# Written order for z and for attention's output product, the last head's outputs split from PSUM, and one conv step per product

## The chip, the cores and the metric

The kernel runs on one core of one Trainium2 chip. The metric is device time in microseconds, the median of three runs. Five engines work side by side and meet through semaphores: PE (TensorE, the matmuls), DVE (VectorE), ACT (ScalarE), POOL (GpSimd) and SP (SyncE, which here only issues transfers). PEld in the profile is PE's loading of stationary operands.

## The reference, cut to what matters

The kernel computes one layer of a decoder block on a sequence of 1024 tokens of width 1024, all in float32: a Mamba-2 branch and a differential-attention branch side by side, merged by gates, and then a gated feed-forward with a causal convolution of width 3.

```python
proj = h @ w_in[layer]
z, xbc, dt_raw, q, k, v, gates = jnp.split(proj, IN_SPLITS, axis=-1)
y_ssd = ssd_branch(z, xbc, dt_raw, ...)      # uses silu(z), dt = softplus(dt_raw + dt_bias), decays exp(cumsum(dt * a))
y_att = diff_attention_branch(q, k, v, ...)  # 8 heads: softmax 1 - lam * softmax 2, times v, then an RMS norm
gate_ssd, gate_att = jnp.split(jax.nn.sigmoid(gates), N_BRANCH, axis=-1)
merged = gate_ssd * (y_ssd @ w_ssd_o[layer]) + gate_att * (y_att @ w_attn_o[layer])
mix = merged @ w_out[layer]
...
u = causal_dwconv(h2 @ w_up[layer], conv_ffn_w[layer], conv_ffn_b[layer])
u_gate, u_val = jnp.split(u, 2, axis=-1)
f = (jax.nn.gelu(u_gate, approximate=True) * u_val) @ w_down[layer]
```

## The kernel before, in words

**Products in three parts.** Every large product keeps float32 accuracy by splitting each operand into a high part (rounded, type `fp32r`) and a low part (what is left), and adding three matmuls: high x high, high x low, low x high. `split(hi, lo, raw)` does this with one ACT instruction (line 93) and one DVE instruction (line 94). `mm3` (lines 112 to 117) issues the three matmuls for each of a list of operand pairs. Raw weights land in three rotating buffers (`wraw`), their high and low parts in four each (`whi`, `wlo`); a buffer is free again when all that reads it is done. PSUM has two double banks for products (`ps_mm`), two single banks `wa` and one each of `wb` and `wc`.

**Who sets the order.** Outside of `tc.manual_schedule(engines=...)` a scheduler orders each engine's instructions by a cost model; within it, the named engines run them in the order in which the program writes them.

**z (lines 522 to 543).** The product for z and dt is cut into three thirds of some 346 columns. A third loads four weight slices (`wz`, two blocks of 128 rows each) and runs eight products of 24 matmuls, one for each 128 tokens. Each product's sixth and last group of matmuls by slice reads slice 3. A product is evacuated by a tanh on ACT (539), a multiply-add on DVE (540) and a store to `zd` (541). POOL works meanwhile on sums of down-projection weights (`down_sums`, lines 411 to 420): two 512 KB loads, four sums, two 512 KB stores, once for every four products. After the first third, `decays` (line 482 on) computes softplus and the decays from the 16 dt columns: a chain of some twenty small DVE steps, then two matmuls (`acum_ps`), exponentials, and eight transposes. All of this is ordered by the scheduler.

**Attention (lines 1126 to 1166).** 64 items (8 heads x 8 query blocks) run in written order on PE, DVE, ACT and POOL; SP is left to the scheduler. For an item, `scores` makes the two score products, `probs` the softmax pair `p` (1069), `transposes` turns `p` (1077) and copies it to `aT` (1078), and `values` multiplies by v (1090). Between these, `fill` emits one piece at a time of other products (here the gate product `gap`), and `run_bg` emits small steps that wait in a list. After every fourth item `norm_o` queues the RMS norm of the outputs (its steps on `sqt` are lines 1099 to 1108) and `out_o` transposes them, scales them to `osb` and stores them to DRAM (`atd`, lines 1117 to 1119).

**Attention's output product.** After the last item come 36 turns with a call of `fill` each (the last 20 pieces; then it has nothing left), the last `out_o` among them. Beside them the 16 parts of the attention output (8 blocks x 2 halves of the tokens) are loaded back from `atd` into `stg` (1178) and split into `oT`, one every second call, the last part only at the end. Then eight output blocks `ao` of 48 matmuls each follow, in scheduler's order: load and split the block's weight (`wao`), in blocks 1, 2 and 6 `early_sums` (load two feed-forward weights, make four sums on DVE, lines 1228 to 1231, and store them from POOL, 1233 and 1234), in blocks 3 to 6 the splits of a quarter of `w_out`, the loads of the gate and the Mamba state, two halves of matmuls, and the merge (`mt`, 1256 and 1257, and the split into `mT`).

**Feed-forward up.** The up product goes by pairs of blocks m, each with seven products p of 12 matmuls (`up_mms`, lines 1356 to 1358) on PSUM banks X, Y and Z, by a scheme with seven products where eight would be usual. Behind each product stand, in written order, sums of banks (`cg`, `cv`, on DVE at 1780, 1789 and 1793; `evs` copies on ACT), sums and splits of coming weights, and steps of the convolution of the block before: `up_conv(m, 0..3)` is a multiply-add over 1022 or 1023 columns on DVE (1374, with an ACT step ahead of every second), `up_conv(m, 4)` the product of gate and value (1378), and `up_gsum(m, 0..3)` four sums of 512 columns (1392). The table `convs` says behind which product (m, p) each stands.

**From up to down.** The down product needs left factors (`left_part`: load and split the stored activations, `g_hi` and `g_lo`) and right factors (`right_part`: load and split weights, `wdb`). The first ones are prepared behind the last up block's products 3 to 6, the later ones in the quarters q of the down product's steps kp.

Of the kernel before, what the change touches and what calls it, by code (L numbers as in the profile page):

```python
# [61 lines left out]
def kernel(ctx: ExitStack, tc: tile.TileContext, a: dict, out: bass.AP, dbg=None):  # L62
# [20 lines left out]
    def ps_wa(name):  # L83
        return pp.tile([P, HALF], F32, tag="wa", name=name, bufs=2)
# [37 lines left out]
    def new_hl(name):  # L122
        return SL.get(name, F32R, (P, 2, HALF))
# [358 lines left out]
    def decays():  # L482
        CH = 8 * NH
        f = lambda t: t.rearrange("p c h -> p (c h)")
# [17 lines left out]
        V.scalar_tensor_tensor(la, dt, -1.0, aexp[:, None, :].broadcast_to([P, 8, NH]), op0=ALU.mult, op1=ALU.mult)  # L502
        pa = ps_wa("acum_ps")
# [10 lines left out]
        V.tensor_tensor(acx[:, :, NH:], acum, hi_r.bitcast(F32), op=ALU.subtract)  # L514
        V.memset(acT.bitcast(F32), 0.0)
# [6 lines left out]
    for c0, wdt in ((0, 346), (346, 346), (692, 348)):  # L522
        wz = [load_moving(a["w_zdt"], 2 * kp, 2, c0, wdt, f"wz{c0}_{kp}") for kp in range(4)]
        for i in range(8):
            ps = ps_mm(f"z{c0}_{i}")[:, 0, :wdt]
            half, q = divmod(i, 4)
            if q == 0:
                down_sums(n_dn)
                n_dn += 1
            tsl = slice(q * P, (q + 1) * P)  # L530
            mm3(ps, [((hT[k][half][:, 0, tsl], hT[k][half][:, 1, tsl]), (wz[k // 2][0][:, k % 2, :], wz[k // 2][1][:, k % 2, :])) for k in range(KD)])
            lo = 0
            if c0 == 0:
                lo = NH
                V.tensor_tensor(dtr[:, i, :], ps[:, :NH], rows[:, R_DTB : R_DTB + NH], op=ALU.add)
            e = ev[n_ev % 2]
            n_ev += 1
            n = wdt - lo
            A.activation(e[:, 0, :n], ps[:, lo:], AF.Tanh, scale=0.5)
            V.scalar_tensor_tensor(e[:, 1, :n], e[:, 0, :n], 1.0, ps[:, lo:], op0=ALU.add, op1=ALU.mult)  # L540
            SP.dma_start(zd[i][:, c0 + lo - NH : c0 + lo - NH + n], e[:, 1, :n])
        if c0 == 0:
            decays()
# [569 lines left out]
    def out_o(j, grp):  # L1113
        need(("norm", j, grp))
        ptr = ps_wb(f"ot{j}_{grp}")
        for qi in range(4):
            T.transpose(ptr[:, qi * P : (qi + 1) * P], ob[:, qi, :], ident)
        A.activation(oe, ptr, AF.Copy, scale=subw)
        SP.dma_start(atd[j][:, grp * HALF : (grp + 1) * HALF], oe)

# [5 lines left out]
    with tc.manual_schedule(engines={EN.PE, EN.DVE, EN.Activation, EN.Pool}):  # L1126
# [6 lines left out]
        for t, (j, i) in enumerate(items):  # L1133
# [28 lines left out]
            emitted["values"] += 1  # L1162
            if j < 7 and i == (4 if j == 0 else 3):
                load_heads(j + 1)
# [5 lines left out]
        SL.put(*thl[0], *thl[1], *qst[0], *kst[0], *klo[0], vt[0], *pt_[0], *qst[1], *kst[1], *klo[1], *pt_[1], vt[1], *aTs)  # L1170

        oT = [[None] * 2 for _ in range(KD)]
        stg = [SL.get(f"stg{i}", F32, (P, 2, HALF)) for i in range(2)]
        parts = [(k, half) for half in range(2) for k in range(KD)]

        def att_in(n):
            k, half = parts[n]
            SP.dma_start(stg[n // 2 % 2][:, n % 2, :], atd[k][:, half * HALF : (half + 1) * HALF])

        def att_split(n):  # L1180
            k, half = parts[n]
            st = stg[n // 2 % 2][:, n % 2, :]
            oT[k][half] = new_hl(f"oT{k}_{half}")
            split(oT[k][half][:, 0, :], oT[k][half][:, 1, :], st)
            if n + 4 < len(parts) - 1:
                att_in(n + 4)

        for n in range(4):
            att_in(n)
        n_att = 0  # L1190
# [9 lines left out]
        while n_att < len(parts) - 1:  # L1200
            att_split(n_att)
            n_att += 1
        att_in(len(parts) - 1)
        att_split(len(parts) - 1)
    SL.put(osb, gev, *stg)
    for k in range(KD):
        SL.put(*hT[k])
    if dbg is not None and "att" in dbg:
        for j in range(8):
            SP.dma_start(dbg["att"][j], atd[j])  # L1210
    if dbg is not None and "ms" in dbg:
        for j in range(8):
            SP.dma_start(dbg["ms"][j], msd[j])


    mT = [[new_hl(f"mT{k}_{h}") for h in range(2)] for k in range(KD)]
    wo = [[None] * 4 for _ in range(2)]
    KH = KD // 2
    fbs = [h * KF + k for k in range(KF) for h in range(2)]

    wsd = [[dp.tile([P, 2, HALF], F32, tag=f"wsd{m}_{i}", name=f"wsd{m}_{i}") for i in range(2)] for m in range(3)]

    def early_sums(m):
        ra, rb = [wp.tile([P, 2, HALF], F32, tag="wraw", name=f"ws{m}_{i}", bufs=3) for i in range(2)]
        for r_, b in ((ra, fbs[m]), (rb, NFF + fbs[m])):
            SP.dma_start(r_.rearrange("p h c -> p (h c)"), a["w_up"][b])
        a11, a12, a21, a22 = ra[:, 0], ra[:, 1], rb[:, 0], rb[:, 1]
        V.tensor_tensor(a22, a21, a22, op=ALU.add)
        V.tensor_tensor(a21, a11, a21, op=ALU.subtract)
        V.tensor_tensor(a11, a22, a11, op=ALU.subtract)  # L1230
        V.tensor_tensor(a12, a12, a11, op=ALU.subtract)
        for i, (x_, y_) in enumerate(((a11, a22), (a21, a12))):
            G.dma_start(wsd[m][i][:, 0], x_)
            G.dma_start(wsd[m][i][:, 1], y_)

    gth = SL.get("gth2")
    mst = SL.get("mst")
    mt = SL.get("mt")
    for j in range(8):
# [3 lines left out]
        if 3 <= j < 7:  # L1243
            kp = j - 3
            raw = wp.tile([P, 2, HALF], F32, tag="wraw", name=f"wo1_{kp}_raw", bufs=3)
            SP.dma_start(raw, a["w_out"][2 * kp * P : (2 * kp + 2) * P, HALF:].rearrange("(k p) c -> p k c", p=P))
            wo[1][kp] = (new_hl(f"wo1_{kp}_hi"), new_hl(f"wo1_{kp}_lo"))
            split(*wo[1][kp], raw)
        ps = ps_mm(f"ao{j}")
        SP.dma_start(gth, gad[j])  # L1250
        SP.dma_start(mst, msd[j])
        for half in range(2):
            block_half(ps[:, half, :], w, oT, half)
        for half in range(2):
            hsl = slice(half * HALF, (half + 1) * HALF)
            V.scalar_tensor_tensor(mt[:, hsl], gth[:, hsl], 1.0, ps[:, half, :], op0=ALU.add, op1=ALU.mult)
            V.tensor_tensor(mt[:, hsl], mt[:, hsl], mst[:, hsl], op=ALU.add)
            split(mT[j][half][:, 0, :], mT[j][half][:, 1, :], mt[:, hsl])
# [231 lines left out]
    with tc.manual_schedule(engines={EN.PE, EN.DVE, EN.Activation, EN.Pool}):  # L1490
# [249 lines left out]
        for (m, p), c in {  # L1740
            (2, 2): (),
            (2, 3): ((0, 2), (0, 3)),
            (2, 4): ((0, 4),),
            (2, 5): ((1, 0),),
            (2, 6): ((1, 1), (1, 2)),
            (3, 0): ((1, 3), (1, 4)),
            (3, 1): (),
            (3, 2): (),
            (3, 3): ((2, 0),),
            (3, 4): ((2, 1), (2, 2)),  # L1750
            (3, 5): ((2, 3),),
            (3, 6): ((2, 4),),
        }.items():
            convs[m, p] = [(up_conv, *x_) for x_ in c]
        convs[3, 1] = [(up_gsum, 1, i) for i in range(2)]
        convs[3, 2] = [(up_gsum, 1, i) for i in range(2, 4)]
        for m in range(2, NPAIR):
# [4 lines left out]
            for p in range(2 if m == 2 else 0, 7):  # L1762
# [183 lines left out]
```

## Time and profile before

| | |
|---|---|
| median of 3 runs | 1925.46 us (1922.19 to 1927.95) |
| profiled execution | 1931.72 us, span 1929.6 us, mean granted TensorE clock 0.994 |
| PE busy | 1868.5 us, 97% of the span, 9128 matmuls |
| DVE, ACT, POOL busy | 1203.8, 852.9 and 214.0 us |
| bytes moved | 310.53 MB, 161 GB/s over the span |
| where the stages lie (us of the span) | z 215 to 325; last scores and probabilities up to 1074; output product 1093 to 1190; early up blocks 1320 to 1380; up to down 1680 to 1720 |

A line of the profile names the source line, the engine, the operation, the output and input by the program's names, and the shapes. In a timeline the first number is the start and the second the time that the instruction, or a group of like ones, took; the bracket tells how long the engine had been idle before, and what it waited for. A row of waits has the total, the number of times and the longest. Rows of instruction groups have busy time and mean duration in ns, and then the idle time before them. Rows of issues have the size and the median time from issue to landing.

### The profile page before, as it was taken

To read this page: it belongs to the slowest core of one execution; us is meant where nothing else is said; L and a number is where in the kernel's file an instruction comes from. 1 tells how busy PE (TensorE), PEld (TensorE's weight loads), DVE (VectorE), ACT (ScalarE), POOL (GpSimd) and SP (SyncE) were. 2 spreads that over 40 slices of the span, in tenths; PEclk is the share of its full clock that TensorE was granted. 3 is DMA by queue.
4 is the path that set the end of the run, shared out by engine and by line. 5 is a ranking of instruction groups with operands and counts; after the bars stand their busy time and mean duration, and the time that the engine had idled before them with its cause. 6 is when DMAs were issued, how large, how long until landed. Compare 5 with 4: busy or idle time off the path is not lost.

```text
span 1929.6 us, 24511 instructions
## 1 busy us (share of the span) xinstructions
PE 1868.5 (97%) x9128; PEld 1556.7 (81%) x9128; DVE 1203.8 (62%) x1815; ACT 852.9 (44%) x1630; POOL 214.0 (11%) x225
## 2 busy tenths in 40 slices
PE   6999989999999999999999899999999999999998
PEld 4787988888888888888888688887788888878886
DVE  6957343575226227767666553468988888886545
ACT  6522123555223115556556432365545455465532
POOL 0000252454451000000000100100000000000001
PEclk9999999999999999999999999999999999999999
DMA  9834364132766846665651776122322232278754
GB/s 303 276 113 148 117 229 164 66 115 88 264 217 142 262 152 178 162 176 160 167 162 58 234 246 207 55 77 77 129 96 104 106 119 93 104 231 282 245 158 158
DMA packets 136151, 310.53 MB, mean 161 GB/s; under 512 B 17120, under 2 KB 48480, under 8 KB 136032
## 3 DMA queue, kind: packets, MB, share of 16 engines
q1 hardware_dynamic: 128384, 282.70, 46.1%
q0 software_dynamic: 7648, 26.26, 4.0%
q8 instruction: 72, 1.18, 0.2%
q14 instruction: 47, 0.39, 0.1%
HBM read 219.49 MB, written 89.41 MB: 160 GB/s over the span
## 4 chain that ended last, share of the span: by engine, by line
PE 82%; DVE 6%; DMA 5%; ACT 4%; issue 2%; SPq 1%; POOL 0%; POOLq 0%; ACTq 0%; DVEq 0%
PE upx L1357 4%; PE upx L1358 4%; PE upx L1356 4%; PE o L1090 3%; PE dx L1720 2%; PE dx L1721 2%; PE dx L1719 2%; PE xbc L117 2%; PE xbc L116 2%; PE xbc L115 2%; PE upy L1357 2%; PE upy L1356 2%; PE upy L1358 2%; PE dy L1721 2%; PE dy L1720 2%; PE dy L1719 2%
## 5 line engine op out<-in xcount | busy, mean ns | idle before, releaser
L1356 PE MATMUL upx<-t,wu_t 128*128 128x512 f32 x264 | 103.4, 392 | 3.4 <-DVE cv L1789 3.0
L1357 PE MATMUL upx<-t,wu_t 128*128 128x512 f32 x264 | 102.9, 390 | 0.2 <-DVE t L1474 0.2
L1358 PE MATMUL upx<-t,wu_t 128*128 128x512 f32 x264 | 102.8, 389 | 0.0
L1078 ACT COPY aT<-at 128x512 f32<-128x512 f32 (+2 forms) x96 | 46.2, 481 | 110.5 <-PE at L1077 110.5
L1330 ACT ACTIVATE wu_t<-sab 128x512 fp32r<-128x512 f32 x57 | 34.0, 627 | 125.7 <-DVE sab L1347 125.7
L1090 PEld LDWEIGHTS o<-vt,aT 128*128 128x128 f32 x576 | 74.8, 191 | 9.5 <-ACT aT L1078 5.3
L1090 PE MATMUL o<-vt,aT 128*128 128x128 f32 x576 | 80.8, 276 | 0.3
L94 DVE TENSOR_TENSOR g_lo<-gst,g_hi 128x1024 fp32r<-128x1024 f32 (+1 forms) x42 | 47.6, 1134 | 49.2 <-ACT g_hi L93 49.2
L142 POOL TENSOR_TENSOR rsf<-rsf,nhalf 128x1 f32<-128x1 f32 x8 | 5.6, 704 | 631.1 <-DVE rsf L141 628.3
L115 PE MATMUL z<-wz_hi,hT 128*128 128x346 f32 (+1 forms) x192 | 63.7, 334 | 9.9 <-ACT wz_hi L93 9.5
L93 ACT ACTIVATE g_hi<-gst 128x1024 fp32r<-128x1024 f32 (+1 forms) x42 | 41.6, 990 | 70.5 <-DMA gst<-gld_s 33.0
L1051 DVE TENSOR_REDUCE nmx<-sc 128x1 f32<-128x640 f32 (+3 forms) x64 | 65.6, 1025 | 2.1
L142 POOL TENSOR_TENSOR sqt<-sqt,nhalf 128x4 f32<-128x4 f32 x16 | 16.5, 1033 | 441.3 <-DVE sqt L141 441.2
L1031 PE MATMUL sc<-kst,qst 128*128 128x512 f32 (+2 forms) x192 | 63.8, 340 | 0.0
L115 PE MATMUL xbc<-hT,wx_hi 128*128 128x512 f32 x160 | 63.5, 397 | 0.0
L116 PE MATMUL z<-wz_lo,hT 128*128 128x346 f32 (+1 forms) x192 | 63.2, 329 | 0.0
L1032 PE MATMUL sc<-klo,qst 128*128 128x512 f32 (+2 forms) x192 | 63.2, 346 | 0.0
L117 PE MATMUL z<-wz_hi,hT 128*128 128x346 f32 (+1 forms) x192 | 62.8, 327 | 0.0
L117 PE MATMUL xbc<-hT,wx_lo 128*128 128x512 f32 x160 | 62.3, 389 | 0.0
L116 PE MATMUL xbc<-hT,wx_hi 128*128 128x512 f32 x160 | 62.2, 389 | 0.0
L1356 PEld LDWEIGHTS upx<-t,wu_t 128*128 128x128 f32 x264 | 49.6, 188 | 15.4 <-DVE cv L1789 4.3
L1374 DVE SCALAR_TENSOR_TENSOR ug<-cg,vec,ug 128x1023 f32<-128x1023 f32 (+1 forms) x44 | 56.3, 1280 | 6.3 <-ACT ug L1373 5.1
(447 smaller groups left out, 5850.5 us busy)
## 6 DMA issues: line engine op xcount, KB each, us to landing
adas<-in_w_ada SPq DMA_DIRECT2D x32, 512.0 KB, 5.1
wdr<-in_w_down POOLq DMA_DIRECT2D x22, 512.0 KB, 6.9
wtd<-wds POOLq DMA_DIRECT2D x22, 512.0 KB, 4.4
wuf<-in_w_up SPq DMA_DIRECT2D x22, 512.0 KB, 3.5
gld_s<-gsum SPq DMA_DIRECT2D x22, 512.0 KB, 2.8
gst<-gld_s SPq DMA_DIRECT2D x20, 512.0 KB, 4.7
wdt_raw<-wtd SPq DMA_DIRECT2D x20, 512.0 KB, 4.5
wuv<-in_w_up SPq DMA_DIRECT2D x19, 512.0 KB, 3.6
```

The costliest lines, as they stand in the source:

```text
L115: T.matmul(ps, lh, rh, start=(i == 0), stop=False)
L116: T.matmul(ps, lh, rl, start=False, stop=False)
L117: T.matmul(ps, ll, rh, start=False, stop=(i == n - 1))
L1031: T.matmul(sc[:, n0:n1], qs_[s][:, tsl], ks_[s][:, n0:n1], start=True, stop=False)
L1051: V.reduce_max(nmx[:, bq, s : s + 1], sc[:, :L], axis=AX.X, negate=True)
L1090: T.matmul(po_of[j, grp][:, qi, :], at[:, k, :], vt[j % 2][:, kt, :], start=(kt == 0), stop=(kt == i))
L1356: T.matmul(out_, wh, xh_, start=(k == 0 and first), stop=False, skip_group_check=not first)
L1357: T.matmul(out_, wh, xl_, start=False, stop=False, skip_group_check=not first)
L1358: T.matmul(out_, wl, xh_, start=False, stop=(k == end), skip_group_check=not first)
L1719: T.matmul(o, gh[:, kk, tsl], wh, start=(k == 0 and not more), stop=False, skip_group_check=more)
L1720: T.matmul(o, gh[:, kk, tsl], wl, start=False, stop=False, skip_group_check=more)
L1721: T.matmul(o, gl[:, kk, tsl], wh, start=False, stop=(k == KF - 1), skip_group_check=more)
```

## The change

- **z.** The z loop is put under written order for PE, DVE, ACT and SP. A third's first three weight slices are fetched behind product 1 of the third before; all four are split behind its product 7, ahead of that product's evacuation, and the fourth is fetched once the first is split. `decays` is cut in three, placed behind products 1, 3 and 5 of the second third.
- **Last head.** At item 55 slots are freed and the loads of stored parts start; from item 57 on, one or two parts are split after each item, ten in all. Head 7 is no longer stored: `out_o` splits its two halves from PSUM. 20 turns are left, four splits stand beside them, and the first output weight is fetched and split there.
- **Output product.** It moves into the written order of PE, DVE, ACT and POOL. Each block's weight is split half a block ahead and fetched one and a half blocks ahead. `early_sums` stands in blocks 0, 1 and 2.
- **Up.** The steps of the convolution for blocks 0 to 4 go one by one behind the 25 products from (2, 3) to (5, 6), with four sums joined to others.
- **Down.** Behind the last up block's products 4, 5 and 6 stand left 0, right 0 and left 1; in the down product, a right part stands in quarter 0 and a left part in quarter 1.

```diff
-    for c0, wdt in ((0, 346), (346, 346), (692, 348)):
-        wz = [load_moving(a["w_zdt"], 2 * kp, 2, c0, wdt, f"wz{c0}_{kp}") for kp in range(4)]
...
+    z_raw = [fetch_z(*thirds[0], kp) for kp in range(3)]
+    with tc.manual_schedule(engines={EN.PE, EN.DVE, EN.Activation, EN.SP}):
+        for t_, (c0, wdt) in enumerate(thirds):
...
+                if t_ < 2 and i == 1:
+                    z_raw = [fetch_z(*thirds[t_ + 1], kp) for kp in range(3)]
+                if t_ < 2 and i == 7:
+                    wz_next = []
+                    for kp in range(4):
+                        wz_next.append(split_z(*thirds[t_ + 1], kp, z_raw.pop(0)))
+                        if kp == 0:
+                            z_raw.append(fetch_z(*thirds[t_ + 1], 3))
...
+                if t_ == 1 and i in (1, 3, 5):
+                    (decays_a, decays_b, decays_c)[i // 2]()
...
+        if j == KD - 1:
+            o = oT[j][grp] = new_hl(f"oT{j}_{grp}")
+            A.activation(o[:, 0, :], ptr, AF.Copy, scale=subw)
+            V.scalar_tensor_tensor(o[:, 1, :], ptr, subw, o[:, 0, :].bitcast(F32), op0=ALU.mult, op1=ALU.subtract)
+            return
...
+            if t == 55:
+                SL.put(*thl[0], *thl[1], *qst[0], *kst[0], *klo[0], vt[0])
+                stg = [SL.get(f"stg{i}", F32, (P, 2, HALF)) for i in range(2)]
+                for _ in range(4):
+                    att_in()
+            elif t > 56:
+                for _ in range(2 if i % 2 else 1):
+                    if n_att < 10:
+                        att_split()
...
-        for n in range(16 + NLAST):
-            if n == 12:
+        for n in range(NLAST):
+            if n == 11:
                 out_o(*pend)
+            if n == 1:
+                fetch_ao(0)
             fill(1)
             run_bg(1)
-            if n % 2 == 1 and n >= 5 and n_att < len(parts) - 1:
-                att_split(n_att)
-                n_att += 1
+            if n % 2 == 1 and n < 9:
+                att_split()
+            if n == 13:
+                split_ao(0)
...
-        w = load_block(a["w_attn_o"][j], f"wao{j}")
-        if j in (1, 2, 6):
-            early_sums(min(j - 1, 2))
...
+        fetch_ao(1)
+        for j in range(KD):
+            w = w_ao.pop(j)
+            ps = ps_mm(f"ao{j}")
+            SP.dma_start(gth, gad[j])
+            SP.dma_start(mst, msd[j])
+            block_half(ps[:, 0, :], w, oT, 0)
+            split_ao(j + 1)
+            fetch_ao(j + 2)
+            if j < 3:
+                early_sums(j, *early_load(j))
...
+            block_half(ps[:, 1, :], w, oT, 1)
...
-        convs = {(m, p): [(up_conv, m - 1, p)] for m in range(3, NPAIR) for p in range(5)}
-        for m in range(4, NPAIR, 2):
+        convs = {(m, p): [(up_conv, m - 1, p)] for m in range(6, NPAIR) for p in range(5)}
+        for m in range(6, NPAIR, 2):
...
-            (2, 3): ((0, 2), (0, 3)),
-            (2, 4): ((0, 4),),
-            (2, 5): ((1, 0),),
-            (2, 6): ((1, 1), (1, 2)),
-            (3, 0): ((1, 3), (1, 4)),
-            (3, 1): (),
-            (3, 2): (),
-            (3, 3): ((2, 0),),
-            (3, 4): ((2, 1), (2, 2)),
...
+        early = [(up_conv, 0, i) for i in range(2, 5)] + [(up_conv, 1, i) for i in range(4)]
+        early = [[x_] for x_ in early] + [[(up_conv, 1, 4), (up_gsum, 1, 0)], [(up_gsum, 1, i) for i in range(1, 4)]]
+        early += [[(up_conv, 2, i)] for i in range(5)] + [[(up_conv, 3, i)] for i in range(4)]
+        early += [[(up_conv, 3, 4), (up_gsum, 3, 0)], [(up_gsum, 3, 1), (up_gsum, 3, 2)], [(up_conv, 4, 0), (up_gsum, 3, 3)]]
+        early += [[(up_conv, 4, i)] for i in range(1, 5)]
+        for n, x_ in enumerate(early):
+            convs[2 + (n + 3) // 7, (n + 3) % 7] = x_
...
-                    if p >= 3:
-                        left_part(0, p - 3)
-                    if p >= 5:
-                        wd[p - 5] = right_part(0, p - 5)
+                    if p in (4, 6):
+                        left_part(0, p // 2 - 2)
+                    elif p == 5:
+                        wd[0] = right_part(0, 0)
...
-                if q == 0 and kp + 4 < KP:
-                    left_part(0, kp + 4)
+                if q == 0 and kp + 1 < KP:
+                    wd[kp + 1] = right_part(0, kp + 1)
                 elif q == 1 and kp + 2 < KP:
-                    wd[kp + 2] = right_part(0, kp + 2)
+                    left_part(0, kp + 2)
```

More of the change, by code (lines that the diff above doesn't have):

```diff
@@ L480, with decays_a @@
     aexp = const("aexp", [P, NH])
[L482 to L484 removed]
+    CH = 8 * NH
+    f = lambda t: t.rearrange("p c h -> p (c h)")
+    def decays_a():
         t0 = f(sp0_)
@@ L520, in decays @@
             V.tensor_copy(acT[:32, half * HALF : (half + 1) * HALF], pt[:32, :])
-    for c0, wdt in ((0, 346), (346, 346), (692, 348)):
-        wz = [load_moving(a["w_zdt"], 2 * kp, 2, c0, wdt, f"wz{c0}_{kp}") for kp in range(4)]
[L524 to L543, printed above, removed]
+    thirds = ((0, 346), (346, 346), (692, 348))
@@ new lines, in fetch_z, with split_z @@
+    def fetch_z(c0, wdt, kp):
+        raw = wp.tile([P, 2, wdt], F32, tag="wraw", name=f"wz{c0}_{kp}_raw", bufs=3)
+        SP.dma_start(raw, a["w_zdt"][2 * kp * P : (2 * kp + 2) * P, c0 : c0 + wdt].rearrange("(k p) c -> p k c", p=P))
+        return raw
+    def split_z(c0, wdt, kp, raw):
+        hi = wp.tile([P, 2, wdt], F32R, tag="whi", name=f"wz{c0}_{kp}_hi", bufs=4)
+        lo = wp.tile([P, 2, wdt], F32R, tag="wlo", name=f"wz{c0}_{kp}_lo", bufs=4)
+        split(hi, lo, raw)
+        return hi, lo
@@ L1169 @@
                 pend = None
[L1170 to L1186, printed above, removed]
@@ L1199 @@
         run_bg(len(bg))
[L1200 to L1239, printed above, removed]
-        w = load_block(a["w_attn_o"][j], f"wao{j}")
-        if j in (1, 2, 6):
-            early_sums(min(j - 1, 2))
[L1243 to L1258, printed above, removed]
+        assert n_att == len(parts)
@@ new lines, with early_load @@
+        SL.put(osb, gev, *stg)
+        for k in range(KD):
+            SL.put(*hT[k])
+        mT = [[new_hl(f"mT{k}_{h}") for h in range(2)] for k in range(KD)]
+        wo = [[None] * 4 for _ in range(2)]
+        KH = KD // 2
+        fbs = [h * KF + k for k in range(KF) for h in range(2)]
+        wsd = [[dp.tile([P, 2, HALF], F32, tag=f"wsd{m}_{i}", name=f"wsd{m}_{i}") for i in range(2)] for m in range(3)]
+        def early_load(m):
+            ra, rb = [wp.tile([P, 2, HALF], F32, tag="wraw", name=f"ws{m}_{i}", bufs=3) for i in range(2)]
+            for r_, b in ((ra, fbs[m]), (rb, NFF + fbs[m])):
+                SP.dma_start(r_.rearrange("p h c -> p (h c)"), a["w_up"][b])
+            return ra, rb
@@ new lines, in early_sums @@
+        def early_sums(m, ra, rb):
+            a11, a12, a21, a22 = ra[:, 0], ra[:, 1], rb[:, 0], rb[:, 1]
+            V.tensor_tensor(a22, a21, a22, op=ALU.add)
+            V.tensor_tensor(a21, a11, a21, op=ALU.subtract)
+            V.tensor_tensor(a11, a22, a11, op=ALU.subtract)
+            V.tensor_tensor(a12, a12, a11, op=ALU.subtract)
+            for i, (x_, y_) in enumerate(((a11, a22), (a21, a12))):
+                G.dma_start(wsd[m][i][:, 0], x_)
+                G.dma_start(wsd[m][i][:, 1], y_)
@@ new lines @@
+        gth = SL.get("gth2")
+        mst = SL.get("mst")
+        mt = SL.get("mt")
+        fetch_ao(1)
[9 more added lines that the diff above has]
+                early_sums(j, *early_load(j))
+            elif j < 7:
+                kp = j - 3
+                raw = wp.tile([P, 2, HALF], F32, tag="wraw", name=f"wo1_{kp}_raw", bufs=3)
+                SP.dma_start(raw, a["w_out"][2 * kp * P : (2 * kp + 2) * P, HALF:].rearrange("(k p) c -> p k c", p=P))
+                wo[1][kp] = (new_hl(f"wo1_{kp}_hi"), new_hl(f"wo1_{kp}_lo"))
+                split(*wo[1][kp], raw)
+            block_half(ps[:, 1, :], w, oT, 1)
+            for half in range(2):
+                hsl = slice(half * HALF, (half + 1) * HALF)
+                V.scalar_tensor_tensor(mt[:, hsl], gth[:, hsl], 1.0, ps[:, half, :], op0=ALU.add, op1=ALU.mult)
+                V.tensor_tensor(mt[:, hsl], mt[:, hsl], mst[:, hsl], op=ALU.add)
+                split(mT[j][half][:, 0, :], mT[j][half][:, 1, :], mt[:, hsl])
```

69 lines of the change are left out of this document (58 added, 11 removed).

## The prediction

> **What bounds the kernel now.** I read the page's busy shares first, then the waits of PE, then counts of matmuls by stretch.
>
> ```profile
> span 1929.6 us, 24511 instructions
> ...
> PE 1868.5 (97%) x9128; PEld 1556.7 (81%) x9128; DVE 1203.8 (62%) x1815; ACT 852.9 (44%) x1630; POOL 214.0 (11%) x225
> ```
>
> TensorE works through 97% of the span, and the change removes no product, so only its 61 us of idle time, and what they cost in clock, can be regained. The waits of PE (what was waited for; total, times, longest) name the places that the change touches:
>
> ```profile
> PE z L115 <- ACT wz_hi L93: 9.5, 2, 5.6
> ...
> PE ao L115 <- ACT oT L93: 4.2, 4, 2.4
> PE at L1077 <- DVE sqt L1099: 3.5, 1, 3.5
> PE upx L1356 <- DVE cv L1789: 3.0, 3, 1.4
> ...
> PE upy L1356 <- ACT evs L1786: 1.2, 3, 0.6
> PE ao L116 <- DVE oT L94: 1.0, 4, 0.4
> PE dx L1720 <- DVE wdb_lo L94: 0.9, 1, 0.9
> ```
>
> These are the z product, the attention tail (rows `sqt` and `ao`), the first feed-forward up products, and the step from up to down. The profiled execution took 1931.7 us, 2.1 more than its span and 6.3 over the median of 1925.5; I work out a difference from its rows and apply it to the median. A measurement of this kernel can tell about 0.3%, 5.8 us, from no change.
>
> A wait row leaves out the slower matmuls behind a wait, so I count matmuls (the number behind PE busy) by stretch. The columns are the stretch, its length, busy time of PE, PEld, DVE, ACT, POOL, granted clock, DMA share, GB/s.
>
> ```profile
> 254.00:256.00 2.00, 2.00 (x8) 2.00 (x8) 1.97 (x2) 0.00 (x0) 2.00 (x3) 0.50 0.61 174
> 273.00:278.00 5.00, 5.00 (x34) 5.00 (x33) 1.03 (x2) 0.53 (x2) 0.40 (x2) 1.00 0.98 320
> 1074.00:1076.00 2.00, 2.00 (x14) 1.69 (x13) 0.21 (x1) 0.59 (x1) 0.55 (x1) 1.00 0.72 284
> 1095.00:1113.00 18.00, 12.86 (x38) 7.91 (x38) 9.65 (x13) 9.89 (x15) 0.00 (x0) 0.81 0.86 293
> 1107.00:1110.00 3.00, 1.82 (x4) 1.45 (x5) 1.84 (x3) 2.38 (x4) 0.00 (x0) 0.50 0.71 259
> 1115.00:1200.00 85.00, 85.00 (x376) 70.38 (x375) 44.61 (x63) 21.96 (x29) 2.18 (x4) 1.00 0.68 230
> 1320.00:1380.00 60.00, 56.44 (x244) 45.12 (x243) 50.18 (x64) 32.79 (x47) 0.00 (x0) 1.00 0.27 94
> 1380.00:1680.00 300.00, 300.00 (x1325) 248.41 (x1324) 253.81 (x334) 149.61 (x220) 0.00 (x0) 1.00 0.30 105
> 1680.00:1720.00 40.00, 37.93 (x164) 30.19 (x164) 31.01 (x37) 20.44 (x28) 0.00 (x0) 1.00 0.65 208
> ```
>
> An undisturbed matmul of 512 columns costs 85/376 = 0.226 us (300/1325 says the same); one of z 5/34 = 0.15. So 1095 to 1113 loses 18 - 38 x 0.226 = 9.4 us; I take 8.7, since a few records may lack. 1320 to 1380 loses 60 - 244 x 0.226 = 4.8, 1680 to 1720 40 - 164 x 0.226 = 2.9.
>
> **The z product.** At its two inner boundaries the fourth weight slice of the next third is late. Here are both waits of PE, then the second boundary's fetch on SP and what POOL issued beside it.
>
> ```profile
> 252.66 0.94 PE L115 MATMUL z<-wz_hi,hT 128*128 128x346 f32 x2 [3.82 <-ACT wz_hi L93]
> ...
> 292.65 0.95 PE L115 MATMUL z<-wz_hi,hT 128*128 128x348 f32 x2 [5.65 <-ACT wz_hi L93]
> ```
>
> ```profile
> 284.02 0.38 SPq L106 DMA_DIRECT2D wz_raw<-in_w_zdt  x1
> ```
>
> ```profile
> 283.19 1.13 POOL L420 DMA_DIRECT2D wtd<-wds  x2
> 284.31 1.06 POOL L412 DMA_DIRECT2D wdr<-in_w_down  x2
> 290.89 1.26 POOL L415 TENSOR_TENSOR wds<-wdr 128x512 f32<-128x512 f32 x1 [5.51 <-DMA wdr<-in_w_down]
> ```
>
> The fetch goes out between POOL's two stores and two loads, 2 MB in all, and the product starts 8.6 us after it. The new code still has three raw buffers, so its fourth fetch still waits for the first slice's split, which waits for product 7: both waits stay. Written order takes away what the scheduler had put into the first wait, six matmuls, 6 x 0.15 = 0.9. And the decay chain now stands whole behind product 1, where it was mixed with evacuations:
>
> ```profile
> 254.84 1.25 DVE L493 TENSOR_TENSOR sm<-sm 128x128 f32<-128x128 f32 x1
> ...
> 261.57 0.29 DVE L499 TENSOR_TENSOR sm<-sm 128x128 f32<-128x128 f32 x1
> ```
>
> ```profile
> 254.62 1.33 POOL L417 TENSOR_TENSOR wds<-wdr,wdr 128x512 f32<-128x512 f32 x1
> ```
>
> Its 20 DVE steps of about 0.3, an exponential and some steps slowed by POOL make 8 to 10 us. Its matmuls stand on PE behind product 3, 48 x 0.15 = 7.2 later, so PE waits 1 to 3 there, and z2's evacuation stands behind the chain on DVE. But PE's arrival at the second boundary sets little: POOL's transfers end near 290.9 whenever PE comes, and a late PE only waits less of the 5.65. Net 0, between -1.5 and +2.5.
>
> A DVE step took 1.25 beside a POOL sum and 0.29 without one. The Trainium skill, "SBUF — State Buffer", section "SBUF: two separate sides", says that a DVE instruction with two SBUF inputs and a GpSimd one that reads SBUF shut each other out for a whole instruction. The trace agrees; by that rule a chain that meets POOL's next four sums is 4 us longer, and the sum below 1 to 2 us worse.
>
> **The last head.** From item 57 on, ten stored parts of the attention output are split between the head's softmax steps; before, two weight splits and the first weight sums stood there.
>
> ```profile
> 1070.19 0.69 DVE L1228 TENSOR_TENSOR ws<-ws 128x512 f32<-128x512 f32 x1 [1.63 <-DMA ws<-in_w_up]
> ```
>
> ```profile
> L94 DVE TENSOR_TENSOR oT<-stg,oT 128x512 fp32r<-128x512 f32 x16 | 10.6, 690 | 11.6 <-ACT oT L93 11.6
> ...
> L93 ACT ACTIVATE oT<-stg 128x512 fp32r<-128x512 f32 x16 | 9.8, 627 | 13.2 <-DMA stg<-atd 13.0
> ...
> L94 DVE TENSOR_TENSOR wao_lo<-wao_raw,wao_hi 128x1024 fp32r<-128x1024 f32 x8 | 9.7, 1218 | 0.3 <-ACT wao_hi L93 0.3
> ...
> L93 ACT ACTIVATE wao_hi<-wao_raw 128x1024 fp32r<-128x1024 f32 x8 | 8.4, 1064 | 18.6 <-PE ao L116 15.6 <-DMA wao_raw<-in_w_attn_o 1.6 <-PE gap L986 1.3
> ```
>
> Ahead of the last probabilities DVE loses two `wao_lo` (2.4), three sums (2.1) and the wait for their data (1.6): 6.1. It gains eight `oT` low parts, 8 x 0.69 = 5.5, and at the end the last output's own low part, 0.7, which holds a PSUM bank that the next transposes want. ACT gains eight high parts, 8 x 0.63 = 5.0, against two `wao_hi`, 2.1. So the 3.5 us wait on `sqt` is not regained; with DVE at 6.1 against 6.2 and ACT 2.9 fuller I take +1. The ends are -3.5 (that wait gone) and +3 (all of ACT's 2.9 in the path of the exponentials).
>
> **Attention's output product.** Its 8.7 us are waits for `oT`, whose parts came too late (13.0 of ACT's idle time before `oT` is put down to `stg`). The issues there, with their median us to landing:
>
> ```profile
> wao_raw<-in_w_attn_o SPq DMA_DIRECT2D x6, 512.0 KB, 4.4
> wsd<-ws POOLq DMA_DIRECT2D x12, 256.0 KB, 3.3
> stg<-atd SPq DMA_DIRECT2D x12, 256.0 KB, 5.8
> ```
>
> The change issues the `stg` loads from item 55 on, eight items ahead, and takes the last head's pair straight from PSUM: all 8.7 go. Late next are weights. The sums of three up blocks now stand, in written order, in output blocks 0 to 2; before, two lay in the head and its fill, one in block 6. Each uses two of three raw buffers, free again when POOL's stores have landed; the next output weight's fetch waits on SP for that, and the next block's gate and state loads stand behind it. DVE runs the sums ahead of the merge steps. One turn: four sums 2.8, stores 3.3, fetch 4.4 to 7 (it is one of five 512 KB loads), high and low part 2.3: 12.8 to 15.4 against 48 x 0.226 = 10.9 of PE work. Three turns fall behind by 1.9 to 4.5 each, with a start some 5 us ahead (weights 0 and 1 are there): 0.7 to 8.5. I take 4, nearer the low end, since the loads' median is the low price. Net -4.7, between -8 and +1.
>
> The clock: z ran at 0.50 (254 to 256) after a wait of 3.82; the tail at 1.00 after the one of 3.50 (1074 to 1076), yet at 0.50 from 1107 after a string of waits none over 2.4. The Trainium skill, "TensorE: Matmul & The Clock Gate", Part 1, says that a window of about 3.4 us without work, which runs freely, halves the clock. The first two rows fit, the third shows that broken work is enough. By the rule, new waits under 3.4 cost no clock, and one of 4 in a piece about 3 us at half speed, 1.5 more: -7.8 instead of the sum below.
>
> **Up, and from up to down.**
>
> ```profile
> L1374 DVE SCALAR_TENSOR_TENSOR ug<-cg,vec,ug 128x1023 f32<-128x1023 f32 x4 | 5.1, 1280 | 0.5 <-ACT ug L1373 0.4
> ```
>
> ```profile
> 1706.33 1.22 DVE L94 TENSOR_TENSOR g_lo<-gst,g_hi 128x1024 fp32r<-128x1024 f32 x1
> 1707.46 0.68 DVE L1789 TENSOR_TENSOR cv<-upx,evs 128x512 f32<-128x512 f32 x1
> ```
>
> A product of 12 matmuls lasts 12 x 0.226 = 2.71. From 1380 to 1680, with about one conv step a product, DVE is busy 253.8 over 1325/12 = 110 products, 2.30 each. A second step of 1.28 makes 3.58, 0.87 too much. In blocks 2 and 3 five products carry two conv steps: 4.4 of the 4.8 lost. The change spreads them one by one as far as block 5. One pair (block 2, product 2) stays, and three products carry a step and a sum (0.69): 2.99, 0.28 too much each. Left 0.87 + 0.84, or 1.6 beside the slack between them; gained 3.2 (1 to 4.7).
>
> In the step to down a left factor's low part, 1.22, stood ahead of the `cv` sum that PE waited for, and others ahead of `wdb_lo`. The change makes left and right parts alternate, some of them a quarter or two later. Of 2.9 I count 2.4, as the third and fourth right parts come just in time (0 to 2.9).
>
> **Sum:** 0 + 1 - 4.7 - 3.2 - 2.4 = -9.3: 1922.4 against the profiled execution, 1916.2 against the median.
>
> **Rivals.** *A, the store chain becomes the bound (slower).* If a fetch behind two other loads lands in 9 and the stores take 4.4, a turn is 2.8 + 4.4 + 9 + 2.3 = 18.5; three fall 22.8 behind, less 5, plus two throttled starts of 1.5: 21 instead of 4, so +7.7, 1933. It is slower than before from 13.3 lost in that product on, a turn of 16. For it: DMA 0.86 busy from 1095 to 1113. Against: medians of 3.3 and 4.4. Chance 0.13. *B, the up losses aren't DVE's order,* and the waits only move: -9.3 + 5.6 = -3.7, 1921.8. For it: the `evs` row waits for ACT. Against: 4.4 of 4.8 explained. Chance 0.10. *C, z gains too:* a fetch out 1 us sooner is ahead of POOL's transfers and lands as `wao_raw` does, in 4.4; with the high part the product starts 3.4 sooner, with no throttle of 1.5: -5 at one boundary, -10 at both, 1906 to 1911. For it: written order takes the next third's other fetches out of SP's queue. Against: the buffer still sets the time. Chance 0.08. *D, the change doesn't do what it says:* the early loads are held on SP by something ahead of them, and `oT` comes as late as before, which hides the weights: -9.3 + 4.7 = -4.6, 1920.9. Against: no buffer wait stands ahead of item 55's loads. Chance 0.04.
>
> **Numbers.** The forecast has 0.65, its own range 1911 to 1923 from the ends of its terms, not all at once. The range 1906 to 1930 takes in B, C and D, and A's milder half. Faster by over 0.3%: 0.56 of the forecast, C, a little of B: 0.65. Within: the rest of the forecast's good half, B, D, part of A: 0.22. Slower: most of A and the forecast's bad ends: 0.13.
>
> **What would show it.** Right: no `ao` wait on `oT`, some on `wao_hi` or `wao_lo`; both z waits on `wz_hi`, the second shorter; a wait of `acum_ps`; a `sqt` wait of 3 to 5; at least 255 matmuls in the stretch that answers to 1320 to 1380. Wrong: `ao` waits over 10 in sum, a z wait gone, or more loss in the up blocks than before.

## The result: 6.5 us slower, and the profile after

The changed kernel takes 1932.95 us (median of 8 runs, 1930.39 to 1937.64) against 1926.43 before (8 runs, 1922.19 to 1930.58): ratio 1.0033, 95% interval 1.0019 to 1.0047. The forecast was 1916.2, 10 us faster. Its profiled execution took 1933.5, span 1931.7.

The waits of PE in the profile of the changed kernel (total, times, longest):

```profile
PE z L115 <- ACT wz_hi L93: 7.5, 2, 4.7
PE acum_ps L507 <- DVE sm L503: 5.3, 1, 5.3
...
PE ao L115 <- ACT wao_hi L93: 4.5, 2, 4.2
...
PE z L116 <- DVE wz_lo L94: 1.7, 2, 1.1
...
PE upx L1419 <- DVE cv L1845: 1.5, 2, 1.3
...
PE at L1112 <- DVE oT L1156: 1.5, 1, 1.5
PE dx L1783 <- DVE wdb_lo L94: 1.3, 1, 1.3
```

The waits on `oT` in the output product and on `sqt` are gone, and `upx` on `cv` halved. New are 4.5 on `wao_hi` and 1.5 on the last output's `oT`, and the wait on `acum_ps` grew from 0.6 to 5.3; both z boundaries still wait, the first 4.7 and 0.65, the second 2.8 and 1.1. Matmuls by stretch of the same profile (length; PE, PEld, DVE, ACT, POOL; clock):

```profile
266.00:274.00 8.00, 2.72 (x17) 2.43 (x16) 7.55 (x14) 0.46 (x1) 6.71 (x8) 0.85 0.30 111
274.00:278.00 4.00, 4.00 (x16) 4.00 (x16) 1.53 (x6) 0.79 (x3) 0.51 (x1) 0.50 0.97 298
...
1143.00:1148.00 5.00, 1.14 (x6) 0.60 (x4) 3.54 (x6) 1.93 (x3) 1.53 (x3) 1.00 0.77 261
1148.00:1152.00 4.00, 3.19 (x8) 2.23 (x9) 1.28 (x2) 0.27 (x1) 0.00 (x0) 0.61 0.89 314
1320.00:1380.00 60.00, 58.23 (x255) 47.23 (x254) 49.08 (x67) 33.20 (x50) 0.00 (x0) 1.00 0.29 98
1700.00:1745.00 45.00, 43.72 (x192) 35.57 (x191) 37.06 (x37) 26.61 (x31) 0.00 (x0) 1.00 0.78 254
```

1320 to 1380 now has 255 matmuls instead of 244. After the `acum_ps` wait PE runs 4 us at half clock, after the `wao_hi` wait at 0.61.

These spans are only 2.1 us apart, where the medians are 6.5 apart. The first experiment shows why: the profile from which the forecast was worked out was a long execution of its kernel.

### The profile page after: what moved, and what is told of

It is laid out like the page before. It is cut to its first block, busy times and chain, and to the rows that moved or that the text cites. A ratio compares the mean times of both kernels' runs of the same rounds, so it can differ in the third digit from the quotient of the medians.

```text
span 1931.7 us, 24508 instructions
## 1 busy us (share of the span) xinstructions
PE 1869.5 (97%) x9128; PEld 1560.1 (81%) x9128; DVE 1209.6 (63%) x1815; ACT 850.4 (44%) x1628; POOL 215.4 (11%) x225
## 4 chain that ended last, share of the span: by engine, by line
PE 80%; DVE 8%; ACT 5%; DMA 4%; issue 2%; SPq 1%; POOL 0%; POOLq 0%; ACTq 0%; DVEq 0%
PE upx L1420 4%; PE upx L1421 4%; PE upx L1419 3%; PE o L1125 3%; PE xbc L115 2%; PE xbc L116 2%; PE xbc L117 2%; PE upy L1420 2%; PE upy L1419 2%; PE upy L1421 2%; PE dx L1783 2%; PE dx L1784 2%; PE dx L1782 2%; PE dy L1784 2%; PE dy L1782 2%
## 5 line engine op out<-in xcount | busy, mean ns | idle before, releaser
L1420 PE MATMUL upx<-t,wu_t 128*128 128x512 f32 x264 | 102.8, 390 | 0.2 <-DVE t L1537 0.2
L1421 PE MATMUL upx<-t,wu_t 128*128 128x512 f32 x264 | 102.8, 389 | 0.0
```

What stands on the lines that cost most here:

```text
L1420: T.matmul(out_, wh, xl_, start=False, stop=False, skip_group_check=not first)
L1421: T.matmul(out_, wl, xh_, start=False, stop=(k == end), skip_group_check=not first)
```

## The experiments

**1. The kernel before, profiled again.**

> The kernel before, unchanged, for a second profile. Its first profile had a span of 1929.6, the changed kernel's 1931.7: 2.1 apart, while the medians are 6.5 apart. If the medians are right, this span is about 1924 to 1927 and some stretch is 3 to 5 us shorter than in the first profile, with the changed kernel's losses unaltered. If the profiles are right, the span is again near 1929.6.

Measured: 1927.69, span 1925.6, 4.0 below the first profile; against this one the changed kernel's span is 6.1 longer, as the medians say. Its waits of PE:

```profile
PE z L115 <- ACT wz_hi L93: 4.8, 1, 4.8
...
PE at L1077 <- DVE sqt L1099: 3.3, 1, 3.3
PE ao L115 <- ACT oT L93: 3.2, 2, 2.4
...
PE ao L116 <- DVE oT L94: 0.2, 1, 0.2
```

z waits once, where the first profile had 3.82 and 5.65, and the output product waits 3.4 instead of 5.2. The second z boundary in this second profile, the fetch on SP and the transfers of POOL (the first profile's rows stand in the prediction):

```profile
284.93 0.38 SPq L106 DMA_DIRECT2D wz_raw<-in_w_zdt  x1
```

```profile
286.01 1.12 POOL L420 DMA_DIRECT2D wtd<-wds  x2
287.12 1.06 POOL L412 DMA_DIRECT2D wdr<-in_w_down  x2
```

The row of its issues says how long it took to land:

```profile
wz_raw<-in_w_zdt SPq DMA_DIRECT2D x1, 348.0 KB, 3.0
```

In the first profile POOL's stores went out at 283.19, 0.8 ahead of the fetch at 284.02, and the same 348 KB took 7.8. Here they come 1.1 behind, and it takes 3.0. The same rows of the changed kernel, where the fetch is 5.5 behind the stores:

```profile
286.07 1.13 POOL L420 DMA_DIRECT2D wtd<-wds  x2
```

```profile
291.55 0.38 SPq L531 DMA_DIRECT2D wz_raw<-in_w_zdt  x1
```

```profile
wz_raw<-in_w_zdt SPq DMA_DIRECT2D x1, 348.0 KB, 5.8
```

Over all profiles of this study that have the three buffers (times from each trace, one execution each; the last column is the time from the first to the last matmul of the z product):

| kernel | POOL's first store | z's fourth fetch | us to landing | z product |
|---|---|---|---|---|
| before, second profile | 286.0 | 284.9 | 3.0 | 102.8 |
| z undone (2) | 284.6 | 283.6 | 2.9 | 102.8 |
| up alone (7) | 285.7 | 284.6 | 2.9 | 101.6 |
| attention alone (9) | 284.9 | 283.8 | 3.0 | 101.5 |
| before, first profile | 283.2 | 284.0 | 7.8 | 108.0 |
| chain in pieces (3) | 284.6 | 285.4 | 7.0 | 109.2 |
| z alone (11) | 285.8 | 287.5 | 7.7 | 112.1 |
| no POOL sums (4) | 282.9 | 287.1 | 5.6 | 109.7 |
| changed kernel | 286.1 | 291.5 | 5.8 | 115.4 |
| sums in block 6 (6) | 284.4 | 291.3 | 4.1 | 112.4 |

With z as before, four of five executions have the fetch about 1 us ahead of POOL, and their z product takes 101.5 to 102.8 us; the fifth, the one of the forecast, has it behind and takes 108.0. In every one with the changed z it is behind.

**2. z left to the scheduler again**, all else as changed.

```diff
-    with tc.manual_schedule(engines={EN.PE, EN.DVE, EN.Activation, EN.SP}):
-        for t_, (c0, wdt) in enumerate(thirds):
...
+    for c0, wdt in ((0, 346), (346, 346), (692, 348)):
+        wz = [load_moving(a["w_zdt"], 2 * kp, 2, c0, wdt, f"wz{c0}_{kp}") for kp in range(4)]
...
+        if c0 == 0:
+            decays_a()
+            decays_b()
+            decays_c()
```

> The changed kernel with the z product and the decays left to the scheduler again, as before. Theory Z (the loss is the z stage: a new wait of 5.3 for the decay chain, slow clock behind it, a second boundary that gains little; by matmul spacing +7.5): 7 to 8 us below the changed kernel, near 1925, so 0 to 6 below the kernel before, since the other parts together gain. Rival O (written order elsewhere costs, z's own loss is made good later): within 3 of the changed kernel, 1930 or more.

Measured: 1923.16, ratio to before 0.9980 (0.9967 to 0.9994). The changed kernel without its z part is faster than before; the z part costs about 10 us (1.0033 - 0.9980, of 1926), above the 7 to 8 expected.

**3. The decay chain in pieces.**

```diff
-        for m in (11, 9, 7, 5, 3, 1):
+        for m in (11, 9, 7):
...
+    def decays_a2():
+        for m in (5, 3, 1):
...
-                if t_ == 1 and i in (1, 3, 5):
-                    (decays_a, decays_b, decays_c)[i // 2]()
+                if t_ == 1 and i in (1, 2, 4, 5):
+                    {1: decays_a, 2: decays_a2, 4: decays_b, 5: decays_c}[i]()
```

> The changed kernel with the decay chain in two pieces, behind products 1 and 2, its two matmuls behind product 4 instead of 3, the rest behind 5. Theory Z: no wait of acum_ps, z2 and z3 evacuated between the pieces, 5 to 7.5 us below the changed kernel, about 1926 to 1928. Rival B (what PE gains in the middle it gives back at the second boundary, since POOL's transfers set when the fourth slice lands): the wait on wz_hi at the second boundary grows from 2.8 to 5 or more, and 1 to 3 us remain.

Measured: 1928.43, ratio to before 1.0000 (0.9980 to 1.0020), some 6 below the changed kernel by the ratios, 5.2 by the spans. The `acum_ps` wait fell from 5.3 to 1.5. The second boundary's waits grew from 2.8 to 4.1: both theories hold, Z for most of it, B for 1 us.

**4. The four POOL sums beside the chain left out.** In the changed kernel DVE's chain and POOL's sums look like this:

```profile
267.12 1.20 DVE L499 TENSOR_SCALAR sm<-sm 128x128 f32<-128x128 f32 x1
268.36 0.29 DVE L498 TENSOR_TENSOR sm<-sm,sm 128x128 f32<-128x128 f32 x1
268.68 1.31 DVE L499 TENSOR_SCALAR sm<-sm 128x128 f32<-128x128 f32 x1
270.03 1.25 DVE L498 TENSOR_TENSOR sm<-sm,sm 128x128 f32<-128x128 f32 x1
271.31 1.17 DVE L499 TENSOR_SCALAR sm<-sm 128x128 f32<-128x128 f32 x1
```

```profile
266.88 1.36 POOL L415 TENSOR_TENSOR wds<-wdr 128x512 f32<-128x512 f32 x1 [8.35 <-DMA wdr<-in_w_down]
268.65 1.26 POOL L416 TENSOR_TENSOR wds<-wdr,wds 128x512 f32<-128x512 f32 x1 [0.41 <-DMA wdr<-in_w_down]
269.87 1.26 POOL L417 TENSOR_TENSOR wds<-wdr,wdr 128x512 f32<-128x512 f32 x1
271.09 1.30 POOL L418 TENSOR_TENSOR wds<-wdr,wds 128x512 f32<-128x512 f32 x1
```

Beside each sum one DVE step takes 1.2 to 1.3 and ends with the sum (267.12 + 1.20 and 266.88 + 1.36); between the sums a step is short again.

```diff
-                    down_sums(n_dn)
+                    down_sums(n_dn, n_dn != 3)
```

The fourth call then only loads and stores: the kernel leaves out four sums that the down product needs.

> The changed kernel without the four POOL sums that ran beside the decay chain (the fourth call's; it stores the loaded weights instead, so part of the down product is left wrong). Theory P (DVE steps beside a POOL sum take 1.2 to 1.3 us instead of 0.23 to 0.29): four steps are short again, the chain from L489 to L503 takes 7.9 instead of 11.9 us and the wait of acum_ps 1.3 instead of 5.3. Rival C (the chain is too long by itself, and POOL only happens to run then): the slow steps stay slow, the wait stays over 4.

Measured: the chain takes 7.9 us (263.4 to 271.3) instead of 11.9, and all its steps between the sums' old places are 0.23 or 0.29:

```profile
PE acum_ps L508 <- DVE sm L504: 1.3, 1, 1.3
```

Theory P holds: four steps, 4.0 us of PE's wait. The z product got shorter with it, 109.7 us instead of 115.4. The time of this single run was 1932.2, hardly below the changed kernel's: its z began 1.5 us later, and 2.9 more were lost behind z, for which nothing here gives a reason.

**5. A buffer of its own for the fourth slice.**

```diff
+    raw4 = SL.get_last("wz_raw4", F32, (P, 2, HALF))
...
                 if t_ < 2 and i == 1:
-                    z_raw = [fetch_z(*thirds[t_ + 1], kp) for kp in range(3)]
+                    z_raw = [fetch_z(*thirds[t_ + 1], kp) for kp in range(3)] + [fetch_z4(*thirds[t_ + 1])]
```

> The changed kernel with a buffer of its own for the fourth weight slice of each third, fetched with the other three behind product 1; the decay chain stays as the change has it. Theory M (the fourth fetch waits for a buffer and then meets POOL's transfers: 5.8 to 7.7 us to landing): both waits on wz_hi and wz_lo go (4.7, 0.65, 2.8, 1.1) with the slow clock behind them, the acum_ps wait of about 5 stays, z's loss by spacing falls from 22.7 to about 10; 10 to 13 us below the changed kernel, about 1921. Rival G (PE is late elsewhere anyway, in the decay chain or the next stage): under 5 us gained.

Measured: 1917.94, ratio to before 0.9958 (0.9943 to 0.9974): 14 below the changed kernel by the ratios, a little above the 10 to 13 expected. Its waits of PE from 210 to 320:

```profile
PE acum_ps L507 <- DVE sm L503: 1.8, 1, 1.8
PE z L116 <- DVE wz_lo L94: 1.3, 2, 0.7
```

The boundaries are nearly closed, and the z product takes 98.1. The `acum_ps` wait fell too, which I had not expected: the chain, from 254.4 to 262.6 there, fell for the most part between two of POOL's rounds (sums up to 257.3 and from 264.0), and no step after the first two was slow.

**6. The third block's sums in output block 6.** The 4.2 us wait in the changed kernel, PE and then ACT:

```profile
1148.33 0.50 PE L115 MATMUL ao<-oT,wao_hi 128*128 128x512 f32 x1 [4.18 <-ACT wao_hi L93]
```

```profile
1143.98 0.63 ACT L93 ACTIVATE mT<-mt 128x512 fp32r<-128x512 f32 x1 [12.12 <-DVE mt L1320]
1146.70 0.63 ACT L93 ACTIVATE mT<-mt 128x512 fp32r<-128x512 f32 x1 [2.08 <-DVE mt L1320]
1147.23 1.04 ACT L93 ACTIVATE wao_hi<-wao_raw 128x1024 fp32r<-128x1024 f32 x1
```

The weight (wao4) was fetched at 1130.7 and took 6.4 to landing: it lay there from 1137.1, ten us before its split. ACT waited 12.1 for the merge of block 2, and DVE for the sums' data ahead of that merge:

```profile
DVE ws L1288 <- DMA ws<-in_w_up: 14.9, 3, 6.6
```

```diff
-            if j < 3:
-                early_sums(j, *early_load(j))
-            elif j < 7:
+            if j in (0, 1, 6):
+                early_sums(min(j, 2), *early_load(min(j, 2)))
+            if 3 <= j < 7:
```

> The changed kernel with the third block's early sums in output block 6 instead of 2. Theory Q (the wait of 4.2 in ao is one of queue order: wao4's high part stands on ACT behind the merge of block 2, that behind the sums of block 2 on DVE, and those wait for a load that POOL's stores held back): the ao waits on wao_hi fall from 4.5 to under 1 with their slow clock, 5 to 7 us below the changed kernel, about 1927. Rival S (the weight itself lands too late because the stores hold its buffer): the wait only shrinks to 2 or 3, or moves to block 3 or 7, under 3 us gained.

Measured: 1926.03, ratio to before 1.0000 (0.9988 to 1.0012), 6 below the changed kernel by the ratios. From 1095 to 1240 PE's waits are

```profile
PE mix L1480 <- ACT mT L93: 1.2, 1, 1.2
PE mix L1482 <- DVE mT L94: 0.6, 1, 0.6
PE ao L117 <- DVE wao_lo L94: 0.4, 1, 0.4
```

Theory Q holds; 1.8 moved on to the next product. The move takes the sums' loads and buffers out of block 2 as well; what speaks against theory S is the landing at 1137.1.

**7. The up steps alone, on the kernel before.** Only the `convs` table is the change's.

> The kernel before with the change's table of convolution steps alone. Theory D (DVE's order in the early up blocks cost 4 to 5 us): 3 to 5 us below the kernel before, the waits upx on cv fall from 3.0 to about 1.5 to 2 (the one at the step to down stays) and upy on evs from 1.4 to under 0.5. Rival: the waits move to other products, no change beyond 1 us.

Measured: 1922.63, ratio 0.9988 (0.9975 to 1.0000), a gain of 2.3 us, not quite clear of nothing: the interval is 0 to 4.8. The 3 to 5 expected lie above the middle, most of them inside it. In its trace `upx` on `cv` falls from 3.0 to 2.1, `upy` on `evs` from 1.4 to 0.6.

**8. The three repairs together** (3, 5 and 6 on the changed kernel).

> The changed kernel with three edits together: the fourth buffer, the decay chain in pieces, the third sums in block 6. If theories Z, M and Q each hold and their gains add, z's loss is 4 to 7, ao has no wait, and the time is about 1908 to 1914, 13 to 20 below the kernel before. If the gains hide one another, 1917 or more.

Measured: 1907.83 (1906.36 to 1908.27), ratio to before 0.9904 (0.9888 to 0.9921): 18 us faster than before, the fastest version found. The gains nearly add: 25 us below the changed kernel by the ratios, where the three by themselves make 27. The waits in z and just behind it (`px` is the next stage's):

```profile
PE px L705 <- DVE sm L710: 2.1, 1, 2.1
PE acT_ps L533 <- DVE sm L526: 0.9, 1, 0.9
PE z L116 <- DVE wz_lo L94: 0.5, 1, 0.5
```

**9. The attention part alone, on the kernel before.**

> The kernel before with the change's last head and output product alone. Theory T (one wait for another: 3 to 4 us on oT and 3.3 on sqt go, about 4.5 on wao_hi, 1.5 on the last output's low part and slow clock come): within 2 us of the kernel before. The prediction's terms for these two parts (+1 and -4.7) say -3.7.

Measured: 1928.81, ratio 1.0015 (1.0001 to 1.0029): 3 us slower, just outside the 2 of theory T, which the interval (0 to 6) includes, and not the -3.7 of the prediction's terms. Waits from its list:

```profile
PE ao L115 <- ACT wao_hi L93: 4.6, 1, 4.6
...
PE at L1084 <- DVE oT L1128: 1.5, 1, 1.5
...
PE mix L1452 <- ACT mT L93: 1.0, 1, 1.0
```

They take the place of 3.3 on `sqt` and 3.4 on `oT` in the second profile of before, and the long one costs clock (0.50 from 1138 to 1142, right behind it).

**10. The fourth buffer on the kernel before.** The edit of 5, in the scheduler's loop.

> The kernel before with a buffer of its own for the fourth weight slice of z, all else as before. Theory M (at the first boundary the fourth fetch always meets POOL's transfers, at the second only where it comes behind POOL's stores): the wait of 4.8 and its slow clock go, and now and then a second one; z's loss falls from 10.5 to about 3 to 5, the time 5 to 8 us below the kernel before, about 1918. Rival (the scheduler has other work to put there, or the loads then collide elsewhere): within 2 us.

Measured: 1923.60, ratio 0.9985 (0.9974 to 0.9996): 2.9 gained, a miss of the 5 to 8. The boundary waits went, and another took their place:

```profile
PE acum_ps L504 <- DVE sm L502: 4.8, 1, 4.8
```

The scheduler's order has an evacuation in the middle of the chain, and that waited for its buffer's store:

```profile
257.76 0.52 DVE L550 SCALAR_TENSOR_TENSOR ev<-ev,z 128x346 f32<-128x346 f32 x1 [4.39 <-DMA zd<-ev]
```

So the wait at the boundary had covered the chain. The buffer pays in full only where the chain no longer stands at the boundary (5, 8).

**11. The z part alone, on the kernel before.**

> The kernel before with the change's z product and decays alone. Theory Z with the second profile of before (z's loss 10.5 before, 22.7 after): 10 to 12 us above the kernel before, near 1936, with the wait of acum_ps near 5 and waits on wz_hi at both boundaries. Rival (z's cost depends on what the rest of the change does): under 6.

Measured: 1936.86, ratio 1.0052 (1.0035 to 1.0069), 10 us slower. Its waits of PE in z:

```profile
PE z L115 <- ACT wz_hi L93: 8.7, 2, 4.7
PE acum_ps L507 <- DVE sm L503: 2.3, 1, 2.3
```

Both boundaries wait. `acum_ps` waits 2.3 instead of the 5 expected: POOL's sums began at 268.3, and only one step of the chain (1.23) met them.

## Why the prediction was wrong, step by step

| term | forecast | shown |
|---|---|---|
| z | 0 (-1.5 to +2.5) | about +10 (2, 11) |
| last head and output product | +1 - 4.7 = -3.7 | +3, interval 0 to +6 (9) |
| up steps | -3.2 | -2.3, interval -4.8 to 0 (7) |
| up to down | -2.4 | -1.4 to -3.2 by the traces |
| sum | -9.3 | +6.5, the whole change measured |

**z is the step that failed.** I wrote that PE's arrival at the second boundary sets little, because POOL's transfers end near 290.9 whenever PE comes, and so set the whole of z to 0. Three things were wrong in it.

First, the wait of 5.65 that should have swallowed any delay was an accident of the one profile. In four of the five profiles of unchanged z the fetch passes 1 us ahead of POOL, lands in 3, and nobody waits for it. Nor is 290.9 a fixed time: POOL's next sum, which waits for its loads, began at 295.28 in the second profile. The sign was in the prediction's own text: that execution was 6.3 over the median, above all eight executions timed with the result and above all but five of the 77 timed executions of that kernel on record, and I applied its differences to the median all the same.

Second, PE comes some 7 us later in the changed kernel, and in all five profiles of changed z with three buffers the fetch falls behind POOL's stores (5.8 to landing in the changed kernel). So the delay isn't absorbed, and the second boundary, which usually costs nothing, waits 3.9 (2.1 to 4.9 in the five). With a buffer of its own the fetch need not wait for that moment, and 14 us went (5; the first boundary's wait is in them).

Third, the decay chain cost more than its 1 to 3: it took 11.9, and PE waited 5.3 and then ran 4 us at half clock. That this delay was not absorbed shows in experiments 3 and 4: with some 4 us less of the wait, the z product takes 109.2 and 109.7 instead of 115.4. The prediction's estimate of 4 us for four POOL sums, worked out beside the Trainium skill's rule in "SBUF — State Buffer", "SBUF: two separate sides", was the 4 us by which I was short (experiment 4). I let the supposed cushion eat it. The part of the rule that I quoted, on steps with two SBUF inputs, covers only one of the four slow steps; three were `TENSOR_SCALAR`, with one.

**The signs did not tell.** Most of what I had named as signs of being right came all the same: waits of `ao` on `wao_hi` and not on `oT`, both z waits with the second shorter, a wait of `acum_ps`, 255 matmuls in the up stretch; only the wait of 3 to 5 on `sqt` did not. A sign without a size could not tell this result from the forecast.

**Rival C was the kernel before.** Its mechanism, a fetch that goes out 1 us ahead of POOL's transfers, was offered with 0.08 as a gain that the change might bring. It was already there in four of the five profiles of unchanged z, and the change lost it.

**The output product.** Forecast: 8.7 out, 4 in. From 1143 to 1152 PE issued 14 matmuls in 9 us, so 9 - 14 x 0.226 = 5.8 came in, where I took 4 (waits of 4.2 and 0.5, and a stretch at 0.61). Out went less, since a usual execution waits 3.4 for `oT` and not 5.2. The mechanism was half right: sums in three successive blocks were too many, but the weight was not late. It lay in its buffer for ten us, and its split stood on ACT behind the merge, the merge on DVE behind the sums, and those waited 6.6 for their own load. The sums' load counted through the order of the engines' queues, not through the weight's fetch, which is where I had priced it.

**The last head.** The wait on `sqt` shrank from 3.5 to 1.5 where I had said that it would stay; in the sum of the attention part (9) nothing of that is left.

**Up and down.** The up term came out a little under its size, and by its reasoning: 255 matmuls in 1320 to 1380, the number named, 2.4 us of loss left instead of 4.8, where I had counted 1.6; by itself it gave 2.3 (7). In the step to down the waits on `cv` in `upx` fell, the one on `wdb_lo` stayed at 1.3. The changed kernel has 192 matmuls from 1700 to 1745, the first profile of before 186:

```profile
1700.00:1745.00 45.00, 42.93 (x186) 34.37 (x185) 35.09 (x35) 25.05 (x29) 0.00 (x0) 1.00 0.79 258
```

The six are 1.4 us; the second profile of before has 178 there, which makes it 3.2. This part was not run by itself. The single parts (+10, +3, -2.3, and -1.4 to -3.2) add to between 7.5 and 9.3 where 6.5 was measured, within their intervals.

**Rival A** named the slower side and a time, 1933, that fits by luck. Its mechanism did not occur: the output product lost 5.8, not 21.

**The clock.** A wait of 5.3 and one of 4.2 were each followed by clock below full (0.50 for 4 us, 0.61 for 4), where 3.5 in one piece was not: this fits the rule of the Trainium skill ("TensorE: Matmul & The Clock Gate", Part 1) that the prediction weighed. By the counts the slow clock added some 1.6 us to the first (16 matmuls in 4 us, where 27 of 0.15 would go) and 1.1 to the second (5.8 less the waits of 4.2 and 0.5).

## What to carry to other kernels

Before a sum is made on a profile, set its own time beside the timed runs: if it lies outside them, some of its waits are accidents, and a second profile of the same kernel is the cheapest experiment there is. A transfer that passes another queue's burst by a microsecond is a state and not a margin: say what happens on either side, and give it a buffer rather than an order. When a stage is put into written order, look where each chain of small steps ends on PE and what DVE shares with POOL at that time; and when one wait is taken away, look which work it had covered.

## What the runs showed of the hardware

- Beside a POOL sum of 1.26 to 1.36 us, one DVE step of 128x128 each took 1.17 to 1.31 instead of 0.23 or 0.29, steps with one source operand (`TENSOR_SCALAR`) as well as with two (changed kernel); without the sums none did (experiment 4).
- A fetch of 348 KB took 2.9 to 3.0 us when issued 1 us ahead of 2 MB of POOL's transfers, 7.0 to 7.8 when issued 0.8 to 1.7 us behind the first of them, and 5.8 to 4.1 when issued 4 to 7 us behind (table of experiment 1).
